# Norm products as chains of four passes, products of ones before two small chains, and steps of four generators set elsewhere, in a two-block float32 network on one core

## The chip, the cores and the metric

One core of one Trainium2 chip runs the whole program. The metric is the device time of one execution in microseconds; less is better. "TensorE" is the engine called PE in the profile, VectorE is DVE, ScalarE ACT, GpSimd POOL and SyncE SP.

## The reference

Two blocks work on 256 tokens of width 1,024, all in float32. The first block has four mixers side by side (retention, gated delta rule, gated linear attention and HGRN, four heads each), a cross attention to a memory of 256 tokens, and a feed forward with a causal convolution of width 3. The second block runs twice: three attentions side by side (latent, dilated, and a sparse one that picks keys by an index score), then a feed forward. Cut to what the change touches:

```python
def _rmsnorm(x, w):
    y = x * lax.rsqrt(jnp.mean(x * x, axis=-1, keepdims=True) + EPS)
    return y * w

def _conv_ffn(h, w_up, conv_w, w_down):                    # three times in all
    u = _causal_dwconv(jnp.matmul(h, w_up), conv_w)         # 1024 -> 2 x 2816
    gate, val = jnp.split(u, 2, axis=-1)
    return jnp.matmul(jax.nn.silu(gate) * val, w_down)      # 2816 -> 1024

def _gated_delta_chunked(q, k, v, beta, g):                 # chunks of 64
    ...
    u_v = lax.linalg.triangular_solve(a_mat, beta[..., None] * v, ...)
    ...

h = h + _hybrid_mixer(_rmsnorm(h, mix_norm_w[l]), ...)
h = h + _memory_cross_attn(_rmsnorm(h, xattn_norm_w[l]), _rmsnorm(mem, mem_norm_w), ...)
h = h + _conv_ffn(_rmsnorm(h, ffn_norm_w[l]), ...)

# sparse attention, per query block: an index score over 8 index heads, top 64 keys
score = jnp.einsum('bqhs,bqh->bqs', jax.nn.relu(dots), wib * idx_scale)
_, sel = lax.top_k(score, k_sel)
```

## The kernel before

Activations lie transposed: features on the 128 partitions, the 256 tokens along the columns, eight tiles for the width of 1,024. A float32 product is made of three: both operands are split into a high and a low part, and `mm_f` (L435 to L437) issues high by high, low by high and high by low into one PSUM bank, each a single pass over 256 columns. `mm_t` (L446 to L448) does the same with the tokens as rows. Products that are not split (`mm`, L457, and the transposes, L461) run on plain float32 and take two passes each.

Weights stream in 512 KB chunks. For each chunk the DMA on SP's queue loads `raw`, ScalarE makes the high part (L416) and VectorE the low part (L417), two chunks ahead of their use and at a higher priority (`PRIO = 42`) than other work on those engines.

A norm (`sumsq`, `mean`, `inv_root`) squares the eight tiles on ScalarE, adds them up on GpSimd (L540), and multiplies the sum by a matrix of ones on TensorE (`psS`, L457 from `mean`), which leaves each token's sum on all partitions. With `join=False` the last square is not added: `mean` then issues a second product of ones for it into the same bank. In `ffn` the first two of the 22 groups of the up projection (`FIRST = 2`) stand ahead of that product, everything else behind it; the result is only needed when the first groups are scaled.

The order of instructions on each engine is made by a scheduler from the order in which the program issues them, their dependences and their priorities. Where several chains run side by side they are Python generators, and `weave` takes one step of each in turn, up to its next `yield`. In the first block two such weaves follow each other: delta, HGRN and projections in turns (L779), then gated linear attention, the memory's norm (`keys_norm`) and retention (L782). `delta` solves its triangular system in five levels: per level a product `psy`, a masked copy `Y` on VectorE (L988), a product `psu`, an addition into `TM`, and a turn `psw` back through the identity. `scan_levels` makes for each of HGRN's levels scaled queries `R` on VectorE (L1133) and the product `psc`. `read_out` (bank `po`) sums a mixer's chunks; retention's comes behind its masked scores `Pm` (L1283). `keys` projects the memory to keys. In the second block a tuple, `ATTN`, sets the order of the attention's steps by hand; each "side" in it advances the top-k generator of the index score by one step, whose products are `psi` (L1619), with a rectifier on ScalarE (L1622) and an addition on VectorE behind them.

Of the kernel before, what the change touches and what calls it, by code (L numbers as in the profile page):

```python
# [22 lines left out]
EPS = 1e-6  # L23
NEG = -1e30
PRIO = 42
FIRST = 2
NZ = 4
LAST = 2
# [6 lines left out]
JOIN = True  # L35
ENG = False
STEP = 8
ATTN = ("kk", "qi0", "prep", "t0", "qi1", "uv", "uq0", "kp", "uq1", "ki", "mkb", "lv0", "uk0", "lv1", "tab", "side", "uq2", "M0",
        "uq3", "uk1", "l0", "Mv0", "M1", "Mv1", "D0", "Dv0", "l1", "l2", "side", "l3", "side", "D1", "Dv1", "side",
        "side", "D3", "side", "Dv3", "side", "D2", "side", "side", "s0", "sides", "Dv2", "s1", "S0", "S1", "Sv0",  # L40
        "Sv1")
MIX_ORDER = ("bq0", "bq1", "bk0", "bk1", "bv0", "bv1", "t0", "t1", "dq0", "dq1", "rq0", "rq1", "rk0", "rk1", "t3", "cq", "ck", "t2", "t4")
# [325 lines left out]
class Net:  # L368
# [87 lines left out]
    def mm(self, out, lhsT, rhs, start=True, stop=True):  # L456
        self.nc.tensor.matmul(out, lhsT, rhs, start=start, stop=stop, skip_group_check=True)  # L457

    def tr(self, out, in_):
        p = in_.shape[0]  # L460
        self.nc.tensor.transpose(out, in_, self.ident[:p, :p])  # L461
# [166 lines left out]
    def ffn(self, tag, g, fc, nt):  # L628
        nc = self.nc
        x = self.x  # L630
        xh, xl = self.xsplit(x, g)
        acc, = self.sumsq(x)
        with self.pool("ffn" + tag) as big, self.pool("fz" + tag, 3) as zp:
            self.pad(big, "g")
            gh = big.tile([P, NFF, T], F32R, name="gh")
# [217 lines left out]
    def delta(self, s, sm, gates):  # L853
# [25 lines left out]
        for t in range(2):  # L879
            for q, src in ((0, sq), (1, sk)):  # L880
                for i in range(2):
                    c = t * 8 + q * 4 + 2 * i
                    self.mm(ps[:, c:c + 2], src[:, i, t * P:(t + 1) * P], self.c1("hind"))
        rr = self.rsqrt(m, ps, 1.0, EPS, 16, "gd").rearrange("p (t q h) -> p t q h", t=2, q=2)
        cat = m.tile([P, 2, 3, 4], F32, name="cat")
        nc.vector.tensor_scalar(cat[:, :, 0, :], rr[:, :, 0, :], 0.125, None, ALU.mult)
        nc.vector.tensor_copy(cat[:, :, 1, :], rr[:, :, 1, :])
# [15 lines left out]
        bv = m.tile([P, 2, 4, 64], F32, tag="v", name="bv", bufs=3)  # L903
        for t in range(2):
            pv = self.pb(T, "psv")
            for i in range(2):
                self.tr(pv[:, i * P:(i + 1) * P], s[:, 4 + i, t * P:(t + 1) * P])
            nc.vector.tensor_mul(bv[:, t], pv.rearrange("p (h v) -> p h v", h=4),
                                 beta[:, t].unsqueeze(2).to_broadcast([P, 4, 64]))
# [68 lines left out]
        for k in range(1, 6):  # L978

            b = 1 << k  # L980
            left = lambda a: a.rearrange("p g (n c d) -> p g n c d", c=2, d=b)[:, :, :, 0, :]
            yield
            py = self.pb(T, "psy").rearrange("p (g n d) -> p g n d", g=8, d=b)
            for g in range(8):
                for r in halves:
                    self.mm(py[r, g], An[r, g // 4, g % 4, r], left(Tm)[r, g])
            Y = m.tile([P, 8, 32], F32, tag="Yl", name="Y")
            nc.vector.tensor_mul(Y, py.rearrange("p g n d -> p g (n d)"),  # L988
                                 self.c1("mko")[:, (k - 1) * 32:k * 32].unsqueeze(1).to_broadcast([P, 8, 32]))
            pu = self.pb(T, "psu2").rearrange("p (g c) -> p g c", g=8)  # L990
            for g in range(8):
                for r in halves:
                    self.mm(pu[r, g, :], Tx[r, g, :], Y[r, g, :])
            nc.vector.tensor_add(left(Tm), left(Tm), pu.rearrange("p g (n d) -> p g n d", d=b))
            yield
            turn(Tx, Tm)
# [34 lines left out]
    def read_out(self, i, Pm, v):  # L1031

        nc, m = self.nc, self.mp
        po = self.pso.tile([P, 2, T], F32, tag="o", name="po")
        for h in range(4):
            c = slice(h * 64, (h + 1) * 64)
            self.mm(po[:, 0, c], Pm[:, 0, h, :], v[:, 0, h, :])
            self.mm(po[:, 1, c], Pm[:, 2, h, :], v[:, 0, h, :], stop=False)
            self.mm(po[:, 1, c], Pm[:, 1, h, :], v[:, 1, h, :], start=False)
# [230 lines left out]
    def retention(self, xh, xl, gates, tmaj):  # L1270
# [7 lines left out]
        for h in range(4):  # L1278
# [3 lines left out]
                self.mm(ps[:, c0:c0 + n], k[r, h // 2, st * P:(st + 1) * P], q[r, h // 2, st * P:T], start=st == 0)  # L1282
            nc.vector.tensor_mul(Pm[:, 0::2, h, :], ps[:, 0:T].rearrange("p (b c) -> p b c", b=2), dec[:, h, :].rearrange("p (b c) -> p b c", b=2))  # L1283
            nc.vector.tensor_mul(Pm[:, 1, h, :], ps[:, T:384], dec[:, h, 0:P])
        self.read_out(0, Pm, vR)


    def keys_norm(self, mem):
        nc = self.nc
        nc.sync.dma_start(mem, self.ap["memT"])  # L1290
        self.pad(self.memp, "m")
        self.mh = self.memp.tile([P, KD, T], F32R, name="mh")
        self.ml = self.memp.tile([P, KD, T], F32R, name="ml")
        g = self.par("memw")
        for k in range(KD):
            self.split(self.mh[:, k, :], self.ml[:, k, :], mem[:, k, :], g[:, k:k + 1])
            if k % 2:
                yield
        acc, = self.sumsq(mem)
        yield  # L1300
        v, L = self.mean(acc, "irv")
        self.mB = self.inv_root(self.st, v, L, "nB")
        yield
        self.mT = self.cols(self.st, self.mB)

    def keys(self):
        nc = self.nc
        self.preload("natural_log_exp_and_others", self.last_silu)
        self.kM = self.memp.tile([P, KD, T], F32, name="kM")
        for i in range(KD):  # L1310
            ps = self.pa(T, "psk")
            self.mm_f(ps, f"wk{i}", range(KD), self.mh, self.ml)
            nc.scalar.copy(self.kM[:, i, :], ps)

    def xattn(self, es):
        nc = self.nc
# [293 lines left out]
    def topk(self, m, qi, ki, wi, sel):  # L1610
# [4 lines left out]
        for h in range(8):  # L1615
# [7 lines left out]
            for t in range(2):  # L1623
                prev = acc[:, sl[t]] if h else (cm[:, P:T] if t == 0 else cm)
                nc.vector.scalar_tensor_tensor(acc[:, sl[t]], rl[:, sl[t]], wi[:, t, h:h + 1], prev, ALU.mult, ALU.add)
            if h % 4 == 3:
                yield
        m8 = m.tile([P, 2, 8], F32, name="m8")
        out = -3.0e38
# [72 lines left out]
```

## Time and profile before

| | |
|---|---|
| median of three runs | 1159.55 us |
| the three runs | 1151.79, 1159.55, 1160.25 us |
| the profiled execution, its own time | 1151.56 us |
| its span in the trace | 1149.8 us, so 1.76 us lie around it |
| TensorE busy | 98% of the span |
| VectorE, ScalarE, GpSimd busy | 81%, 58%, 10% |
| mean granted clock of TensorE | 0.994 |
| read from memory | 182.07 MB, 159 GB/s over the span |

The trace gives each instruction's start and duration. Matmuls are pipelined, so a duration (0.28 us for a single pass of 256 columns) is longer than the distance to the next start; rates are read from starts or from counts in a window. A count x2 on a product of one call is its number of passes. PEclk is the granted clock as a share of the full 2.4 GHz.

### The profile page before, as it was taken

What the parts mean: (1) busy time and instruction counts of PE and PEld (TensorE: products, weight loads), DVE (VectorE), ACT (ScalarE), POOL (GpSimd) and SP (SyncE); (2) the same over time, 40 slices, a digit from 0 to 9 for tenths busy, and PEclk for the clock granted to TensorE, in tenths of its full rate; (3) what the DMA queues carried; (4) which work ended last, traced back from release to release, by engine and by line L of the source; (5) the groups of instructions that cost most, each with busy time, mean ns of one, the idle gap of its engine ahead of it and who ended that gap; (6) DMA issues with size and microseconds to landing.
All of it is one profiled execution on the core that took longest, in us unless ns stands there. A gap on an engine that the chain in (4) does not pass through costs nothing.

```text
span 1149.8 us, 23781 instructions
## 1 busy us (share of the span) xinstructions
PE 1124.8 (98%) x9452; PEld 1079.7 (94%) x9452; DVE 927.7 (81%) x1867; ACT 666.2 (58%) x1173; POOL 112.4 (10%) x139
## 2 busy tenths in 40 slices
PE   8899999999999999999999999999999999999996
PEld 8788888989999999999989999999999899999996
DVE  6977769587589997659997899986679979999854
ACT  6653545466576665555555676665555547666642
POOL 7401201010010000223000200001220002000000
PEclk9999999999999999999999999999999999999999
DMA  7513142556456555554424556555553235555552
GB/s 256 181 57 109 40 152 72 182 182 217 130 166 199 188 187 192 185 172 150 140 93 128 166 202 201 188 198 193 180 172 119 94 129 170 198 189 192 188 184 85
DMA packets 52095, 184.66 MB, mean 161 GB/s; under 512 B 6032, under 2 KB 6928, under 8 KB 51728
## 3 DMA queue, kind: packets, MB, share of 16 engines
q1 hardware_dynamic: 51264, 181.90, 48.6%
q8 instruction: 74, 1.21, 0.4%
q0 software_dynamic: 144, 0.59, 0.2%
q10 hardware_dynamic: 576, 0.66, 0.2%
q14 instruction: 37, 0.30, 0.1%
HBM read 182.07 MB, written 1.05 MB: 159 GB/s over the span
## 4 chain that ended last, share of the span: by engine, by line
PE 87%; DVE 7%; ACT 2%; DMA 1%; issue 1%; POOL 1%; SPq 0%; DVEq 0%; ACTq 0%; POOLq 0%
PE psU L437 11%; PE psU L435 11%; PE psU L436 11%; PE psD L435 5%; PE psD L436 5%; PE psD L437 5%; PE po L457 3%; PE psp L435 3%; PE psp L436 3%; PE psp L437 3%; PE psW L435 3%; PE psW L437 3%; PE psW L436 2%; DVE wlo L417 2%; PE pss L457 2%; PE pst L448 2%
## 5 line engine op out<-in xcount | busy, mean ns | idle before, releaser
L416 ACT ACTIVATE whi<-raw 128x1024 fp32r<-128x1024 f32 (+5 forms) x411 | 362.5, 898 | 298.3 <-PE psU L436 59.6
L417 DVE TENSOR_TENSOR wlo<-raw,whi 128x1024 fp32r<-128x1024 f32 (+5 forms) x411 | 425.6, 1048 | 133.2 <-ACT whi L416 130.3
L435 PE MATMUL psU<-xh,whi 128*128 128x256 f32 x1056 | 295.4, 280 | 0.0
L437 PE MATMUL psU<-xh,wlo 128*128 128x256 f32 x1056 | 295.0, 279 | 0.3 <-DVE wlo L417 0.3
L436 PE MATMUL psU<-xl,whi 128*128 128x256 f32 x1056 | 294.8, 279 | 0.0
L437 PEld LDWEIGHTS psU<-xh,wlo 128*128 128x128 f32 x1056 | 201.0, 190 | 0.5 <-DVE wlo L417 0.5
L436 PEld LDWEIGHTS psU<-xl,whi 128*128 128x128 f32 x1056 | 198.4, 188 | 0.1
L435 PEld LDWEIGHTS psU<-xh,whi 128*128 128x128 f32 x1056 | 198.2, 188 | 0.1
L437 PE MATMUL psD<-gh,wlo 128*128 128x256 f32 x528 | 147.5, 279 | 0.0
L435 PE MATMUL psD<-gh,whi 128*128 128x256 f32 x528 | 147.5, 279 | 0.0
L436 PE MATMUL psD<-gl,whi 128*128 128x256 f32 x528 | 147.5, 279 | 0.0
L540 POOL TENSOR_TENSOR ssa<-ssa,ssq 128x256 f32<-128x256 f32 x61 | 56.6, 932 | 692.4 <-ACT ssq L538 428.6
L673 DVE SCALAR_TENSOR_TENSOR y<-zb,prm,y 128x256 f32<-128x256 f32 x264 | 114.2, 480 | 0.0
L437 PEld LDWEIGHTS psD<-gh,wlo 128*128 128x128 f32 x528 | 100.6, 191 | 0.0
L436 PEld LDWEIGHTS psD<-gl,whi 128*128 128x128 f32 x528 | 99.1, 188 | 0.0
L435 PEld LDWEIGHTS psD<-gh,whi 128*128 128x128 f32 x528 | 99.1, 188 | 0.0
L435 PE MATMUL psp<-xh,whi 128*128 128x256 f32 (+1 forms) x288 | 83.5, 290 | 0.0
L436 PE MATMUL psp<-xl,whi 128*128 128x256 f32 (+1 forms) x288 | 82.4, 286 | 0.0
L437 PE MATMUL psp<-xh,wlo 128*128 128x256 f32 (+1 forms) x288 | 82.1, 285 | 0.0
L664 ACT ACTIVATE y<-zb,prm 128x256 f32<-128x256 f32 x132 | 67.3, 558 | 5.7 <-DVE zb L660 5.5
L446 PE MATMUL pst<-whi,xh 128*128 128x256 f32 (+3 forms) x176 | 56.9, 323 | 2.0 <-ACT gates L774 1.6
L435 PEld LDWEIGHTS psp<-xh,whi 128*128 128x128 f32 (+1 forms) x288 | 54.3, 188 | 2.4 <-issue 2.3
(452 smaller groups left out, 2305.4 us busy)
## 6 DMA issues: line engine op xcount, KB each, us to landing
raw<-in_wst_dram SPq DMA_DIRECT2D x319, 512.0 KB, 3.5
raw<-in_wst_dram SPq DMA_DIRECT2D x5, 448.0 KB, 3.3
cst<-in_c_dram SPq DMA_DIRECT2D x1, 1664.0 KB, 7.2
raw<-in_wst_dram SPq DMA_DIRECT2D x3, 396.0 KB, 3.0
mem<-in_memT_dram SPq DMA_DIRECT2D x1, 1024.0 KB, 6.1
raw<-in_wst_dram SPq DMA_DIRECT2D x2, 480.0 KB, 3.1
raw<-in_wst_dram SPq DMA_DIRECT2D x2, 420.0 KB, 3.5
raw<-in_wst_dram SPq DMA_DIRECT2D x2, 384.0 KB, 4.2
```

Source lines behind the costliest of these rows:

```text
L416: nc.scalar.activation(hi[:, a:b], raw[:, a:b], AF.Copy)
L417: nc.vector.tensor_sub(lo[:, a:b], raw[:, a:b], hi[:, a:b].bitcast(F32))
L435: nc.tensor.matmul(ps, wh, xh[:, k, :], start=s, stop=False, skip_group_check=True)
L436: nc.tensor.matmul(ps, wh, xl[:, k, :], start=False, stop=False, skip_group_check=True)
L437: nc.tensor.matmul(ps, wl, xh[:, k, :], start=False, stop=e, skip_group_check=True)
L446: nc.tensor.matmul(pss[t], xh[:, k, a], wh, start=i == 0, stop=False, skip_group_check=True)
L448: nc.tensor.matmul(pss[t], xh[:, k, a], wl, start=False, stop=i == n - 1, skip_group_check=True)
L457: self.nc.tensor.matmul(out, lhsT, rhs, start=start, stop=stop, skip_group_check=True)
L540: (eng or nc.gpsimd).tensor_add(acc, acc, sq)
L664: nc.scalar.activation(y[:, e, u, :], z[:, e, 2:], AF.Identity, scale=fc[:, c + 2:c + 3], **kw)
L673: nc.vector.scalar_tensor_tensor(y[:, e, u, :], zs[u][:, e, j:j + T], fc[:, c + j:c + j + 1], y[:, e, u, :], ALU.mult, ALU.add)
```

## The change

Seven edits, none of which changes a projection. In each of the three feed forwards the sum of squares is taken with `join=False`: one addition on GpSimd less, and a second product of ones. Delta's reciprocal root gets a priority of its own (`URGENT = 200`). A helper `hum` issues products of the ones matrix by itself into a bank that the next product overwrites: four ahead of delta's first transposes of values (`psv`), three ahead of retention's read-out (`po`). Delta's level gets a third `yield`, behind `Y`; retention gets one ahead of its read-out. `keys_norm` yields at every tile, and its sum of squares, mean and root move into `keys`, behind the first, fifth and seventh tile of keys. The top-k generator yields at every second index head (before: every fourth), and `ATTN` has two more "side" steps.

```diff
+URGENT = 200
@@
-ATTN = (... "tab", "side", "uq2", "M0",
-        "uq3", "uk1", "l0", ...
+ATTN = (... "tab", "side", "uq2", "side", "M0",
+        "uq3", "side", "uk1", "l0", ...
@@
+    def hum(self, ps, n):
+        for _ in range(n):
+            self.mm(ps[:, 0:P], self.ones, self.ones)
@@ def ffn
-        acc, = self.sumsq(x)
+        acc, = self.sumsq(x, join=False)
@@ def delta
-        rr = self.rsqrt(m, ps, 1.0, EPS, 16, "gd").rearrange("p (t q h) -> p t q h", t=2, q=2)
+        with self.tc.high_priority(offset=URGENT):
+            rr = self.rsqrt(m, ps, 1.0, EPS, 16, "gd").rearrange("p (t q h) -> p t q h", t=2, q=2)
@@
             pv = self.pb(T, "psv")
+            if t == 0:
+                self.hum(pv, 4)
@@
             nc.vector.tensor_mul(Y, py.rearrange("p g n d -> p g (n d)"), ...)
+            yield
             pu = self.pb(T, "psu2").rearrange("p (g c) -> p g c", g=8)
@@ def read_out
         po = self.pso.tile([P, 2, T], F32, tag="o", name="po")
+        if i == 0:
+            self.hum(po[:, 0], 3)
@@ def retention
+        yield
         self.read_out(0, Pm, vR)
@@ def keys_norm
+        self.mem = mem
...
             self.split(self.mh[:, k, :], self.ml[:, k, :], mem[:, k, :], g[:, k:k + 1])
-            if k % 2:
-                yield
-        acc, = self.sumsq(mem)
-        yield
-        v, L = self.mean(acc, "irv")
-        self.mB = self.inv_root(self.st, v, L, "nB")
-        yield
-        self.mT = self.cols(self.st, self.mB)
+            yield
@@ def keys
-        self.preload("natural_log_exp_and_others", self.last_silu)
+        pl = self.preload("natural_log_exp_and_others", self.last_silu)
...
             nc.scalar.copy(self.kM[:, i, :], ps)
+            if i == 0:
+                acc, = self.sumsq(self.mem)
+            elif i == 4:
+                self.pl = pl
+                v, L = self.mean(acc, "irv")
+                self.mB = self.inv_root(self.st, v, L, "nB")
+                self.pl = None
+            elif i == 6:
+                self.mT = self.cols(self.st, self.mB)
@@ def topk
-            if h % 4 == 3:
+            if h % 2:
                 yield
```

The change shifts the line numbers by one from the first edit on and by more behind the later ones. Three places in TensorE's order show what moves.

TensorE at the norm of the first feed forward, before (`psU` is the up projection, `psS` the product of ones):

```order
L436 MATMUL psU<-xl,whi 128x256
L437 MATMUL psU<-xh,wlo 128x256
L457 MATMUL psS<-ssa,ones 128x256
L435 MATMUL psU<-xh,whi 128x256
L436 MATMUL psU<-xl,whi 128x256
```

And now:

```order
L437 MATMUL psU<-xl,whi 128x256
L438 MATMUL psU<-xh,wlo 128x256
L458 MATMUL psS<-ssa,ones 128x256
L458 MATMUL psS<-ssq,ones 128x256
L436 MATMUL psU<-xh,whi 128x256
L437 MATMUL psU<-xl,whi 128x256
```

The second product of ones, for the last square, stands right behind the first; the stream of single passes around them is the same.

TensorE at the start of delta, before (`psr` turns the roots, `pse` spreads them, `psv` are the transposes of the values, `psq` and `pst` projections):

```order
L448 MATMUL pst<-wlo,xh 128x512
L435 MATMUL psq<-xh,whi 128x256
L436 MATMUL psq<-xl,whi 128x256
L461 MATMUL psr<-ident,cat 12x128 x2
L437 MATMUL psq<-xh,wlo 128x256
L435 MATMUL psq<-xh,whi 128x256
L436 MATMUL psq<-xl,whi 128x256
L437 MATMUL psq<-xh,wlo 128x256
L457 MATMUL pse<-rows,cst_142 128x256 x6
L461 MATMUL psv<-ident,s 128x128 x2
L435 MATMUL psq<-xh,whi 128x256
L461 MATMUL psv<-ident,s 128x128 x2
```

And now:

```order
L448 MATMUL pst<-whi,xl 128x512
L467 MATMUL psr<-ident,cat 12x128 x2
L449 MATMUL pst<-wlo,xh 128x512
L436 MATMUL psq<-xh,whi 128x256
L437 MATMUL psq<-xl,whi 128x256
L438 MATMUL psq<-xh,wlo 128x256
L436 MATMUL psq<-xh,whi 128x256
L437 MATMUL psq<-xl,whi 128x256
L438 MATMUL psq<-xh,wlo 128x256
L458 MATMUL pse<-rows,cst_142 128x256 x6
L458 MATMUL psv<-ones 128x128 x4
L467 MATMUL psv<-ident,s 128x128 x4
```

The turn of the roots now stands ahead of all of these `psq` products (before, behind two of them), so that six of them lie between it and `pse` instead of four; four products of ones stand ahead of the transposes, which follow each other without a projection between. Further on, delta's last three `psu`, two of its `psy` and three `psw` now stand with HGRN's `psc` and `psl` with only two `pst` products among them; before, runs of `psr` and `pst` lay between most of them.

TensorE in the first attention of the second block, where the index scores `psi` meet the latent projections `psp`, before:

```order
L448 MATMUL pst<-wlo,xh 128x256
L1619 MATMUL psi<-ki,qi 128x128
L1619 MATMUL psi<-ki,qi 128x256
L1619 MATMUL psi<-ki,qi 128x128
L1619 MATMUL psi<-ki,qi 128x256
L1619 MATMUL psi<-ki,qi 128x128
L1619 MATMUL psi<-ki,qi 128x256
L1619 MATMUL psi<-ki,qi 128x128
L1619 MATMUL psi<-ki,qi 128x256
L435 MATMUL psp<-lath,whi 128x256
```

And now:

```order
L449 MATMUL pst<-wlo,xh 128x256
L1635 MATMUL psi<-ki,qi 128x128
L1635 MATMUL psi<-ki,qi 128x256
L1635 MATMUL psi<-ki,qi 128x128
L1635 MATMUL psi<-ki,qi 128x256
L436 MATMUL psp<-lath,whi 128x256
L437 MATMUL psp<-latl,whi 128x256
L438 MATMUL psp<-lath,wlo 128x256
L436 MATMUL psp<-lath,whi 128x256
L437 MATMUL psp<-latl,whi 128x256
L438 MATMUL psp<-lath,wlo 128x256
L1635 MATMUL psi<-ki,qi 128x128
```

The products of four index heads, two each, stood in a row; now six projection products lie between the first two heads and the next two.

## Rows read from the trace of the kernel before

**Rows 1.** The page: busy time of each engine, its share, and instructions.
```profile
PE 1124.8 (98%) x9452; PEld 1079.7 (94%) x9452; DVE 927.7 (81%) x1867; ACT 666.2 (58%) x1173; POOL 112.4 (10%) x139
```

**Rows 2.** Windows: us, busy PE, PEld, DVE, ACT, POOL (x instructions), PEclk, DMA share, GB/s.
```profile
30.00:220.00 190.00, 182.10 (x1606) 161.31 (x1607) 149.88 (x358) 99.73 (x208) 26.68 (x31) 0.97 0.33 107
...
638.00:828.00 190.00, 190.00 (x1671) 189.80 (x1670) 160.18 (x233) 120.71 (x170) 15.75 (x19) 1.00 0.59 191
```

**Rows 3.** Windows, psU alone: us, PE, PEld, DVE, PEclk, DMA share, GB/s.
```profile
333.00:433.00 100.00, 100.00 (x851) 100.00 (x850) 13.23 (x20) 1.00 0.58 190
656.00:756.00 100.00, 100.00 (x885) 100.00 (x884) 13.04 (x19) 1.00 0.59 193
970.00:1070.00 100.00, 100.00 (x852) 100.00 (x850) 12.32 (x18) 1.00 0.57 189
```

**Rows 4.** Timeline of PE: start us, us, engine, line, operation, passes; around 514.53.
```profile
511.70 0.28 PE L435 MATMUL psp<-xh,whi 128*128 128x256 f32 x1
...
514.53 1.02 PE L457 MATMUL psS<-ssa,ones 128*128 128x256 f32 x4
...
515.51 0.28 PE L436 MATMUL psp<-xl,whi 128*96 128x256 f32 x1
...
515.98 0.28 PE L437 MATMUL psp<-xh,wlo 128*96 128x256 f32 x1
...
518.02 0.28 PE L437 MATMUL psp<-xh,wlo 128*96 128x256 f32 x1
```

**Rows 5.** Timeline of PE at the norms of the first and second feed forward.
```profile
330.36 0.59 PE L457 MATMUL psS<-ssa,ones 128*128 128x256 f32 x2
...
330.91 0.28 PE L436 MATMUL psU<-xl,whi 128*128 128x256 f32 x1
...
651.43 0.59 PE L457 MATMUL psS<-ssa,ones 128*128 128x256 f32 x2
```

**Rows 6.** Timeline of PE in the last attention.
```profile
901.09 0.93 PE L457 MATMUL pss<-rk,rq 64*128 64x128 f32 x8
...
902.75 0.28 PE L435 MATMUL psp<-xh,whi 128*128 128x256 f32 x1
...
904.34 0.28 PE L437 MATMUL psp<-xh,wlo 128*128 128x256 f32 x1
```

**Rows 7.** Windows at the two low clocks (columns as in rows 2).
```profile
53.30:60.10 6.80, 6.42 (x23) 5.15 (x22) 4.86 (x10) 0.76 (x2) 1.49 (x3) 0.50 0.23 77
131.80:135.20 3.40, 3.40 (x11) 2.45 (x10) 3.27 (x12) 0.00 (x0) 1.77 (x3) 0.50 0.00 0
```

**Rows 8.** Waits of PE: line waited for, us in total, times, longest us.
```profile
PE psi L1619 <- ACT irl L1622: 2.2, 3, 1.0
...
PE psc L457 <- DVE R L1133: 1.3, 2, 0.9
...
PE psu L457 <- DVE Y L988: 0.8, 2, 0.5
...
PE po L457 <- DVE Pm L1283: 0.7, 1, 0.7
PE psr L461 <- DVE cat L888: 0.6, 1, 0.6
```

**Rows 9.** Timeline of DVE and POOL at the memory's norm.
```profile
124.56 0.49 DVE L1133 TENSOR_TENSOR R<-qbD,Ehalf 128x128 f32<-128x128 f32 x2
...
127.07 5.62 POOL L540 TENSOR_TENSOR ssa<-ssa,ssq 128x256 f32<-128x256 f32 x7 [13.48 <-ACT ssq L538]
...
128.77 0.82 DVE L1133 TENSOR_TENSOR R<-qbD,Ehalf 128x128 f32<-128x128 f32 x1
```

**Rows 10.** Timeline of PE at one of delta's levels.
```profile
96.71 1.12 PE L457 MATMUL psy<-TM,An 64*64 64x32 f32 x32
...
100.34 1.12 PE L457 MATMUL psu<-Y,TM 64*64 64x32 f32 x32 [0.48 <-DVE Y L988]
```

More of the change, by code (lines that the diff above doesn't have):

```diff
@@ L37 @@
 STEP = 8
-ATTN = ("kk", "qi0", "prep", "t0", "qi1", "uv", "uq0", "kp", "uq1", "ki", "mkb", "lv0", "uk0", "lv1", "tab", "side", "uq2", "M0",
-        "uq3", "uk1", "l0", "Mv0", "M1", "Mv1", "D0", "Dv0", "l1", "l2", "side", "l3", "side", "D1", "Dv1", "side",
+ATTN = ("kk", "qi0", "prep", "t0", "qi1", "uv", "uq0", "kp", "uq1", "ki", "mkb", "lv0", "uk0", "lv1", "tab", "side", "uq2", "side", "M0",
+        "uq3", "side", "uk1", "l0", "Mv0", "M1", "Mv1", "D0", "Dv0", "l1", "l2", "side", "l3", "side", "D1", "Dv1", "side",
         "side", "D3", "side", "Dv3", "side", "D2", "side", "side", "s0", "sides", "Dv2", "s1", "S0", "S1", "Sv0",
```

## The prediction

> **What bounds the kernel now.** I read the busy line first. TensorE is busy 1,124.8 of 1,149.8 us [rows 1], so whatever the change gains has to come out of TensorE's own time: out of products that take longer than they need, or out of the 25 us in which it stands. The windows by stage come next [rows 2]. The stretch from 30 to 220 us holds the mixers and most of the edits; there TensorE stands 190.00 - 182.10 = 7.9 us, and its granted clock is 0.97. The stretch from 638 to 828 us is mostly a feed forward; there it does not stand at all and the clock is 1.00. The feed forwards therefore can't gain from waits.
>
> The third view is the same 100 us inside each of the three feed forwards [rows 3]. All three are 100% busy at clock 1.00 on the same kind of product (one pass, 256 columns), yet they start 851, 885 and 852 of them: 117.5, 113.0 and 117.4 ns each. That is two discrete spacings, not noise. Where the spacing changes is seen at the norm product of the second block [rows 4]: from 511.70 to 514.53 us there are 24 starts, 2.83 / 24 = 117.9 ns; then comes a chain of two products of ones, four passes; from 515.98 to 518.02 there are 18 starts, 113.3 ns. A product of two passes does it less reliably [rows 5]: the first feed forward's, at 330.36, was left wide, the second's, at 651.43, short. A chain of eight passes before a projection also ends short [rows 6]: 902.75 to 904.34, 14 starts, 113.6 ns. I read this as a spacing that any disturbance of the stream sets anew and that then stays: a single product of two passes sets it by luck, a chain of four and more mostly sets it short.
>
> **The change part by part**, against the profiled execution's own 1151.56 us (span 1149.8 and 1.76 around it). That execution is the fastest kind shown: the three runs read 1151.79, 1159.55 and 1160.25. The 8 us between the first and the other two are, as an estimate, little more than one feed forward in the other spacing (6.7, below), so I take the sum from this execution and compare the result with the median, 1159.55.
>
> A. Spacing in the feed forwards. The second product of ones makes the last disturbance of each feed forward a chain of four passes, like that of rows 4. A feed forward has 22 x 2 x 8 x 3 = 1,056 up products and 8 x 22 x 3 = 528 down products; 96 of them (two of 22 groups) stand ahead of the norm, 1,488 behind. By rows 3 the difference is 117.5 - 113.0 = 4.5 ns, so 6.7 us each. The first and third go from wide to short, the second is short already: -13.4. The bounds are 0 and -13.4. I take -13.4 since the one chain of this very form in the trace (rows 4) turned wide into short. Whether weights arrive in time at the shorter spacing is answered by the second feed forward: 885 products at a DMA share of 0.59 and TensorE still 100% busy [rows 3].
>
> B. Added products. From the norm product's start to the second single product behind it is 0.98 us with four passes (514.53 to 515.51, rows 4) and 0.55 with two (330.36 to 330.91, rows 5): +0.43 per feed forward, +1.3. The dropped POOL add, its last in each norm, only lets the norm product be ready earlier; TensorE does not wait there. The seven products ahead of delta's values and the first read-out are 14 passes of 128 columns; eight passes of 128 columns took 0.93 with their tail [rows 6], about 0.11 each, so +1.5 at full clock and +3.0 at half (bounds 0, where they fill a wait, and 3.0). They wait for the bank that the products behind them need anyway, so they bring no wait of their own, but all of TensorE's queue stands behind them. Together +2.8.
>
> C. Waits. The ones that the moved steps touch are five [rows 8]. The indexer's products (psi) wait 2.2 us for ACT's rectifier to empty a bank. The changed order puts six projection products, 6 x 0.113 = 0.7 us, between the first two index heads and the next two; three waits of up to 1.0 lose most of that: -1.5. The four of the mixers are 1.3 (psc behind R), 0.8 (psu behind Y), 0.7 (po behind Pm), 0.6 (psr behind cat), sum 3.4. The R waits come while POOL makes the seven adds of the memory norm: R takes 0.25 us apiece at 124.56 and 0.82 at 128.77, inside the adds of 127.07 to 132.69 [rows 9]. The change moves these adds into the memory keys' stream, where TensorE has 64 x 3 long products in hand. The root chain ahead, the extra step behind Y and the step ahead of the read-out each put other work in the gap of its own wait. I take -2.5 of 3.4. What is late next is delta itself: with an extra step per level the scan advances faster and eats the projections that stood between delta's later levels, so +1.0 of new waits. Sum -3.0; bounds -5.6 (all five gone) and +5 (none gone, and new ones of the size of the old).
>
> On rows 9 the Trainium skill ("SBUF — State Buffer", section "SBUF: two separate sides") says that VectorE and GpSimd share a port pair as an exclusive lock, which the one that starts first holds for its whole instruction. Row and rule agree (0.25 against 0.82), and the rule speaks against the move: beside the keys the adds block the weight conversions instead, up to the adds' own 5.6 us of VectorE. By it C would be -3.0 + 5.6 = +2.6 at worst; I leave it out of the sum because conversions run ahead of the products.
>
> D. Clock. Twice the granted clock falls to 0.50, the 1.2 GHz level: 53.3 to 60.1 and 131.8 to 135.2 us [rows 7], in both cases after TensorE had stood or run few and small products (the root's wait; the R waits). Half of each stretch is lost: 3.4 + 1.7 = 5.1. The added products of ones stand right at the first, and the moved adds take away the cause of the second. Bounds -5.1 and, since every shift of small work can also open a new dip of that size, +3.4; I take half, -2.5.
>
> Everything else (keys' norm products, the top-k steps, the retention step) is the same work in other places, at 0, hidden by a TensorE that is full around it; no DMA moves with these steps (the memory's load stays where it was). If that cover were gone, the two norm products and two transposes of the memory would cost the 0.55 us of rows 5 twice, 1.1.
>
> Sum: -13.4 + 2.8 - 3.0 - 2.5 = -16.1, so 1135.5 us.
>
> **The rivals.**
>
> Only one of the two wide feed forwards turns short, or the second turns wide while two turn short: -6.7 instead of -13.4, 1142.2 us. For it: a product of two passes left either spacing, and rows 4 are one case only.
>
> The second product does not act on the spacing (it is set elsewhere, or the same luck goes on): A is 0, time 1148.9. [...] Against this rival also speaks that the change of spacing in rows 4 falls exactly on the chain.
>
> The chain sets the wide spacing, everywhere: nothing gained, and the second feed forward loses its short one, 1148.9 + 6.7 = 1155.6.
>
> The slow side: delta's last levels. In the changed order three levels and half of the scan stand in a row with hardly a projection between: some 13 pieces like the 1.12 us psu of rows 10, and 2.4 us of scan products (estimate), 17 us. Between psy (ends 97.83) and psu (100.34) a level's values need 2.5 us to come back from VectorE [rows 10]; a 1.1 us piece covers less than half, so eight hand-overs may each wait 1.4, 11 us, and such a stretch is just what went before the dips of rows 7: at half clock another 17. 1135.5 + 28 = 1164, slower than the 1159.55 median. It decides from 24 us of loss on. Against it: the scan's own waits in this trace are 1.3 and 0.8 in sum [rows 8], and VectorE is relieved there.
>
> The added products of ones do not hold the clock: D is 0, 1138.0; it lies in the forecast's range.
>
> **How the numbers follow.** Forecast 0.50 and its variant without D 0.03; one feed forward only 0.20; no effect on the spacing 0.15; wide everywhere 0.05; delta's levels 0.07. The range goes down to 1129 (all of C, D and no cost of the products of ones would give 1151.56 - 13.4 + 1.3 - 5.6 - 5.1 = 1128.8) and up to 1150, which takes in the case without an effect on spacing. A measurement of this kernel can tell about 1%, 11.6 us, from no change, so faster means below 1147.9, against the median of 1159.55: the first two cases and most of a third of the no-effect case, less what C may give back, 0.74; same 0.21; slower 0.05.
>
> **What would show it.** Right: some 885 psU products per 100 us in all three feed forwards, at 113 ns, each behind a psS of four passes; psi and psc gone from the head of TensorE's waits; clock 1.00 from 50 to 61 and around 130 us. Wrong: 851 per 100 us in a feed forward behind a four-pass psS kills A; new waits of psu, psw or psy or a clock of 0.50 where delta's levels run is the slow rival.

## The result

The change is faster by 1.2%: 1144.26 us, median of four runs (1141.30 to 1146.34), against 1158.9 us before (four runs, 1151.79 to 1160.25); ratio 0.9884, 95% interval 0.9838 to 0.993. The profiled execution took 1141.30 us, 10.3 less than the one profiled before. Ratios, here and below, leave out executions more than 1.5% above the fastest of their kernel, so that they can differ from the ratio of the medians. The forecast of 1135.5 was too far, its range of 1129 to 1150 held, and in the profiles the gain is its term A. The other six edits together gave nothing.

The busy line of the page after, against [rows 1]:

```profile
PE 1113.3 (98%) x9472; PEld 1067.9 (94%) x9472; DVE 926.7 (81%) x1867; ACT 666.6 (58%) x1173; POOL 109.8 (10%) x136
```

TensorE has 20 instructions more and 11.5 us less busy time: its products became shorter in distance, not fewer. Where, the windows of `psU` show, which answer to [rows 3] (us, PE, PEld, DVE, clock, DMA share, GB/s):

```profile
333.00:433.00 100.00, 100.00 (x885) 100.00 (x884) 13.61 (x20) 1.00 0.61 194
656.00:756.00 100.00, 99.66 (x880) 99.46 (x878) 13.03 (x19) 1.00 0.61 197
970.00:1070.00 100.00, 99.68 (x880) 99.48 (x878) 13.00 (x19) 1.00 0.60 194
```

All three feed forwards now run at 113 ns; before, two of the three stood at 851 and 852. The weights arrive in time for it (DMA share 0.60 against 0.58). The norm's chain in the first feed forward (timeline of PE; against the first two of [rows 5]):

```profile
330.51 0.28 PE L438 MATMUL psU<-xh,wlo 128*128 128x256 f32 x1
330.62 0.59 PE L458 MATMUL psS<-ssa,ones 128*128 128x256 f32 x2
331.06 0.59 PE L458 MATMUL psS<-ssq,ones 128*128 128x256 f32 x2
331.30 0.47 PE L436 MATMUL psU<-xh,whi 128*128 128x256 f32 x1
```

The waits, against [rows 8] (us in total, times, longest):

```profile
PE psc L458 <- DVE R L1132: 1.4, 1, 1.4
...
PE psr L458 <- DVE Pm L1296: 1.0, 1, 1.0
...
PE psr L467 <- DVE cat L895: 0.8, 1, 0.8
...
PE psi L1635 <- ACT irl L1638: 0.4, 1, 0.4
```

The index scores wait 0.4 us instead of 2.2, and `psu` behind `Y` is gone from the list. But other waits took the places: the `R` of the other scan's last level (L1132; the line that was L1133 is L1145 now, and waits 0.3) 1.4, the retention scores behind `Pm` 1.0 (before, the read-out behind it 0.7), the roots' turn 0.8 (0.6).

To see where the time went, each execution was cut at the starts of some of TensorE's instructions in its trace: the first `pse`, the first `psy`, the first `psW` (the mixers' output), the first `psU` and last `psD` of each feed forward. A column gives the length from the place before it (the first from the span's start); "FFN" runs from the first `psU` to the last `psD`, "attention" from there to the next `psU`. Lengths in us, worked out from these starts, one execution a row:

| kernel | to pse | to psy | to psW | to psU | FFN 1 | attention | FFN 2 | attention | FFN 3 |
|---|---|---|---|---|---|---|---|---|---|
| before | 51.3 | 17.9 | 144.0 | 104.6 | 188.2 | 133.5 | 181.0 | 131.2 | 187.9 |
| after | 53.0 | 17.5 | 142.1 | 105.4 | 182.0 | 134.2 | 181.0 | 132.4 | 181.7 |
| after_again | 54.1 | 18.8 | 142.0 | 105.7 | 182.0 | 135.9 | 181.0 | 132.2 | 181.7 |
| ffn_only | 51.7 | 17.5 | 143.8 | 105.6 | 188.8 | 133.4 | 181.0 | 133.1 | 182.1 |
| no_ffn | 53.0 | 18.6 | 142.0 | 105.5 | 188.2 | 134.9 | 187.1 | 132.0 | 187.9 |
| ffn_halves | 53.5 | 18.5 | 147.4 | 104.2 | 188.0 | 133.4 | 180.6 | 132.8 | 181.3 |
| no_hum | 54.3 | 18.8 | 140.0 | 104.4 | 182.0 | 136.0 | 188.0 | 132.1 | 181.7 |
| old_attn | 52.8 | 17.5 | 142.2 | 105.7 | 182.1 | 133.4 | 181.0 | 133.5 | 181.7 |
| old_keys | 53.9 | 18.7 | 140.2 | 105.5 | 188.8 | 134.7 | 188.0 | 132.2 | 188.7 |
| no_y_step | 53.8 | 18.5 | 146.2 | 105.5 | 182.1 | 133.8 | 181.0 | 132.7 | 181.7 |
| ffn_six | 53.9 | 17.5 | 142.3 | 105.3 | 182.4 | 134.2 | 181.4 | 132.1 | 182.1 |
| ffn_eight | 52.7 | 17.5 | 142.1 | 105.8 | 182.9 | 134.2 | 181.8 | 132.8 | 182.5 |
| mix_hum | 53.0 | 18.2 | 140.0 | 105.5 | 182.0 | 133.2 | 181.0 | 133.0 | 181.7 |
| mix | 54.7 | 17.8 | 138.5 | 104.9 | 182.0 | 133.2 | 181.0 | 130.9 | 181.7 |

Between the first two rows: 12.4 us less in the feed forwards, 1.9 less in the mixers' stretch ("to psW"), 4.1 more in the others. The six kernels whose mixers are those of the whole change agree within 0.3 us in the mixers' stretch (142.0 to 142.3). The start, the stretch to psy and the first attention differ by 1.1 to 1.7 us between after and after_again, which are the same code, so a difference of that size in one of these is not told from chance.

### The profile page after: what moved, and what is told of

It reads as the page before. It is cut to its first block, busy times and chain, and to the rows that moved or that the text cites. A ratio compares the mean times of both kernels' runs of the same rounds, so it can differ in the third digit from the quotient of the medians.

```text
span 1139.5 us, 23807 instructions
## 1 busy us (share of the span) xinstructions
PE 1113.3 (98%) x9472; PEld 1067.9 (94%) x9472; DVE 926.7 (81%) x1867; ACT 666.6 (58%) x1173; POOL 109.8 (10%) x136
## 4 chain that ended last, share of the span: by engine, by line
PE 84%; DVE 11%; ACT 2%; DMA 1%; issue 1%; POOL 0%; SPq 0%; DVEq 0%; ACTq 0%
PE psU L438 10%; PE psU L436 10%; PE psU L437 10%; PE psD L438 5%; PE psD L436 5%; PE psD L437 5%; DVE wlo L418 4%; PE po L458 3%; PE psW L436 3%; PE psW L438 3%; PE psW L437 2%; PE psp L436 2%; PE psp L438 2%; PE psp L437 2%; PE pst L449 2%; PE pst L447 2%
## 5 line engine op out<-in xcount | busy, mean ns | idle before, releaser
L436 PE MATMUL psU<-xh,whi 128*128 128x256 f32 x1056 | 292.1, 277 | 0.0
L438 PE MATMUL psU<-xh,wlo 128*128 128x256 f32 x1056 | 291.6, 276 | 0.3 <-DVE wlo L418 0.3
L437 PE MATMUL psU<-xl,whi 128*128 128x256 f32 x1056 | 291.5, 276 | 0.0
L438 PEld LDWEIGHTS psU<-xh,wlo 128*128 128x128 f32 x1056 | 198.2, 188 | 0.5 <-DVE wlo L418 0.5
L546 POOL TENSOR_TENSOR ssa<-ssa,ssq 128x256 f32<-128x256 f32 x58 | 53.1, 920 | 681.1 <-ACT ssq L544 459.5
L670 ACT ACTIVATE y<-zb,prm 128x256 f32<-128x256 f32 x132 | 67.4, 560 | 11.5 <-DVE zb L666 11.3
L449 PE MATMUL pst<-wlo,xh 128*128 128x256 f32 (+3 forms) x176 | 55.0, 316 | 1.3 <-DVE wlo L418 1.3
```

Source lines behind the costliest of these rows:

```text
L436: nc.tensor.matmul(ps, wh, xh[:, k, :], start=s, stop=False, skip_group_check=True)
L437: nc.tensor.matmul(ps, wh, xl[:, k, :], start=False, stop=False, skip_group_check=True)
L438: nc.tensor.matmul(ps, wl, xh[:, k, :], start=False, stop=e, skip_group_check=True)
L449: nc.tensor.matmul(pss[t], xh[:, k, a], wl, start=False, stop=i == n - 1, skip_group_check=True)
L546: (eng or nc.gpsimd).tensor_add(acc, acc, sq)
L670: nc.scalar.activation(y[:, e, u, :], z[:, e, 2:], AF.Identity, scale=fc[:, c + 2:c + 3], **kw)
```

## The experiments

Two theories. The spacing: the second product of ones makes the gain. Its rival: the edits in the mixers and the attention make it. And against the reason for the spacing: that it is luck.

**The second product alone, and all but it.** `ffn_only` is the kernel before with one edit, `no_ffn` the whole change without it.

```diff
 # ffn_only: only this; no_ffn: everything but this
-        acc, = self.sumsq(x)
+        acc, = self.sumsq(x, join=False)
```

> The kernel before with one edit of the change, the second product of ones in the three feed forwards. If the spacing behind a chain of four passes is the gain: some 885 psU products per 100 us in all three feed forwards, a profiled time near 1151.6 - 13.4 + 1.3 = 1139.5 us, so no slower than the whole change (1141 to 1146). If the gain came from the mixers and the attention: 1150 to 1160, with 851 per 100 us in one feed forward at least.

> The whole change without the second product in the feed forwards. If the spacing is the gain: the feed forwards fall to either spacing by chance, 1141 to 1142 - 1.3 plus 6.7 for each wide one, so 1146 to 1160 and a spread of several us between executions; at three wide ones no faster than before. If the gain came from the other edits: 1140 to 1146, whatever the spacing.

> The whole change once more on this chip, to compare with the others: 1141 to 1146 us; 885 psU products per 100 us in all three feed forwards if the four passes set the spacing, 851 in one of them now and then if it is luck.

Measured: ffn_only 1145.84 us (1139.93 to 1149.04; ratio to before 0.9893, 0.986 to 0.9926), no_ffn 1162.31 (1154.41 to 1164.93; 1.0038, 1.0013 to 1.0064), after_again 1143.67 (1141.55 to 1145.38; 0.9872, 0.9837 to 0.9907). One edit gives what all seven give, and the other six alone are a little slower than before. The windows of psU in no_ffn:

```profile
333.00:433.00 100.00, 100.00 (x851) 100.00 (x850) 13.02 (x19) 1.00 0.56 189
656.00:756.00 100.00, 100.00 (x851) 100.00 (x850) 13.00 (x19) 1.00 0.55 188
970.00:1070.00 100.00, 99.92 (x848) 99.72 (x847) 12.24 (x18) 1.00 0.56 188
```

Wide in all three. But the expectation for ffn_only failed in one place; its windows:

```profile
333.00:433.00 100.00, 100.00 (x851) 100.00 (x850) 13.02 (x19) 1.00 0.55 188
656.00:756.00 100.00, 100.00 (x885) 100.00 (x884) 13.52 (x20) 1.00 0.57 193
970.00:1070.00 100.00, 100.00 (x884) 100.00 (x884) 13.60 (x20) 1.00 0.57 194
```

Its first feed forward stayed wide behind a chain of four passes. So a chain of four does not simply set the short spacing. The stream had turned wide 6 us ahead of the chain, where TensorE waits for a weight's low part (timeline of PE):

```profile
324.34 0.28 PE L437 MATMUL psU<-xh,wlo 128*128 128x256 f32 x1
...
325.25 0.28 PE L436 MATMUL psU<-xl,whi 128*128 128x256 f32 x1
325.81 0.39 PE L437 MATMUL psU<-xh,wlo 128*128 128x256 f32 x1 [0.29 <-DVE wlo L417]
326.03 0.28 PE L435 MATMUL psU<-xh,whi 128*128 128x256 f32 x1
...
327.09 0.28 PE L435 MATMUL psU<-xh,whi 128*128 128x256 f32 x1
```

From 324.34 to 325.25 are eight starts of 0.114 us, from 326.03 to 327.09 nine of 0.118. By their starts, eleven of the fourteen profiles have this gap with a short stream ahead of it: the stream turned wide there in ffn_only and old_keys and stayed short in the other nine. So the gap can turn it, and does not always.

**Four passes without a second operand.** `ffn_halves` is the kernel before with the one product of the feed forwards cut in two (`cut` is 2 there, 1 elsewhere).

```diff
-            self.mm(ps, self.ones, a, start=i == 0, stop=i == len(acc) - 1)
+            for c in range(cut):
+                b = slice(c * T // cut, (c + 1) * T // cut)
+                self.mm(ps[:, b], self.ones, a[:, b], start=i == 0, stop=i == len(acc) - 1)
```

> The kernel before; in the feed forwards the one product of ones is cut into two of 128 columns, so that four passes stand there with the same work and no second operand. If four passes set the short spacing: 885 per 100 us in all three, near 1139 us, less than ffn_only by the passes saved (0.4 us each). If 256 columns or the second operand are needed: 851 per 100 us in some, 1150 to 1160.

Measured: 1144.79 us (1139.76 to 1151.73; 0.9892, 0.9851 to 0.9933). Behind all three chains the spacing was short at first; in the first feed forward it turned wide 11 us later, behind a gap of 0.2 us (timeline of PE):

```profile
347.71 0.28 PE L436 MATMUL psU<-xl,whi 128*128 128x256 f32 x1
347.91 0.39 PE L437 MATMUL psU<-xh,wlo 128*128 128x256 f32 x1
348.14 0.28 PE L435 MATMUL psU<-xh,whi 128*128 128x256 f32 x1
...
348.96 0.28 PE L436 MATMUL psU<-xl,whi 128*128 128x256 f32 x1
```

From 348.14 to 348.96 are seven starts of 0.117 us. A short gap can come with a change of spacing too; one of 0.22 us at 348.56 in no_y_step left it short. Neither a second operand nor 256 columns are needed for the chain: three streams that came in short left four passes of 128 columns short. And the profiled execution's 1151.73 comes from this gap and from a mixers' stretch of 147.4, in which the clock was lower (5.0 us lost between 150 and 175).

**The edits beside it.** Four kernels, each the whole change without one edit.

```diff
 # no_hum
-            if t == 0:
-                self.hum(pv, 4)
-        if i == 0:
-            self.hum(po[:, 0], 3)
 # old_attn: ATTN as before, and
-            if h % 2:
+            if h % 4 == 3:
 # old_keys: keys_norm and keys as before
 # no_y_step, in delta's level
-            yield
             pu = self.pb(T, "psu2")
```

> The whole change without the seven products of ones. If these hold the clock (term D): the granted clock falls to 0.50 near 53 to 60 us for longer, and the stretch from pse to the first psy grows from 17.5 to 18.8 us by one or more. If they only cost: that stretch shrinks by about 1.5 and the time by as much, 1142.

> The whole change with the attention order and the top-k steps of before. If those edits gave the 1.5 us of psi waits: the two attention stretches (end of psD to the next psU; 134.2 to 135.9 and 132.0 to 132.4 with the change) grow by 0.7 each. If they cost more elsewhere: the stretches shrink to before's 133.5 and 131.2, and the time falls by 2 to 3 us, 1141.

> The whole change with the memory's norm back in keys_norm. If moving it gave the gain in the mixers: the stretch from the first psy to the first psW grows from 142.0 to 144 us, with R waits of 1 us and more and a clock of 0.50 near 130 us. If it is the step behind Y that gave it, the stretch stays at 142.

> The whole change without the extra step behind Y in delta's levels. If that step gave the gain in the mixers: the stretch from the first psy to the first psW goes from 142.0 back to 144 us. If it costs (the rival on delta's last levels): 141 or less. If the keys' move gave the gain: 142 stays.

Medians: no_hum 1145.91 us (1138.30 to 1155.24; ratio 0.9925, 0.9877 to 0.9973), old_attn 1141.60 (1140.65 to 1142.51; 0.9892, 0.9836 to 0.9948), old_keys 1154.07 (1138.70 to 1162.81; 0.9951, 0.9901 to 1.0002), no_y_step 1153.46 (1146.52 to 1160.70; 0.9994, 0.9954 to 1.0034). These medians mix the edit with the spacing, which moves a run by 6.7 us per feed forward: old_keys' profiled execution had all three wide, no_hum's one. The stretches tell the edits apart.

The extra step behind `Y` is the one of the edits tried that gains: without it the mixers' stretch is 146.2 instead of 142.0 us. The view of DVE and POOL in no_y_step shows why; against [rows 9]:

```profile
128.79 0.48 DVE L1144 TENSOR_TENSOR R<-qbD,Ehalf 128x128 f32<-128x128 f32 x2
...
131.29 5.63 POOL L546 TENSOR_TENSOR ssa<-ssa,ssq 128x256 f32<-128x256 f32 x7 [13.49 <-ACT ssq L544]
...
133.00 0.82 DVE L1144 TENSOR_TENSOR R<-qbD,Ehalf 128x128 f32<-128x128 f32 x1
```

The seven adds of the memory's norm stand beside the R exactly as before, although the keys' move is in this kernel. In the whole change (same view) the R are over before the adds begin:

```profile
108.97 1.30 DVE L1145 TENSOR_TENSOR R<-qbD,Ehalf 128x128 f32<-128x128 f32 x6 [0.54 <-PE psl L458]
...
115.04 4.15 POOL L546 TENSOR_TENSOR ssa<-ssa,ssq 128x256 f32<-128x256 f32 x5
```

Six R in 1.30 us, 0.22 each. So the step behind Y, which lets the scan run ahead of delta, parted R and adds; the keys' move left the adds where they were (in old_keys, without the move, they run at 117.10 us, behind the R as well). The waits of no_y_step bear it out:

```profile
PE psc L458 <- DVE R L1144: 2.1, 4, 0.9
...
PE psu L458 <- DVE Y L997: 1.2, 2, 0.9
```

The keys' move costs: with the old keys the stretch is 140.2 instead of 142.1 (140.0 in mix_hum, below). It brings the wait of 1.4 us for R of L1132, which stands, at 1.4 each time, in the lists of all eight kernels with the moved keys and in none of the six with the old ones. DVE and POOL at that place in the whole change:

```profile
183.53 4.05 POOL L798 TENSOR_TENSOR gates<-gates,prm 128x512 f32<-128x512 f32 x3 [61.10 <-ACT gates L795]
...
186.37 1.76 DVE L1132 TENSOR_TENSOR R<-qbC,Ehalf 128x512 f32<-128x512 f32 x1
```

And in old_keys:

```profile
187.43 4.86 POOL L798 TENSOR_TENSOR gates<-gates,prm 128x512 f32<-128x512 f32 x3 [62.95 <-ACT gates L795]
...
188.41 1.04 DVE L1132 TENSOR_TENSOR R<-qbC,Ehalf 128x512 f32<-128x512 f32 x1
```

The same R takes 1.76 us where it starts 2.8 us into POOL's three products and 1.04 where it starts 1.0 us into them; with no product on POOL the other scan's took 0.68 (at 113.32 us in the whole change). That the overlap is the cause was not tried by itself.

The products of ones cost 2.1 us in the mixers' stretch (142.1 with, 140.0 without; with the keys and the attention of before, in mix_hum and mix below, 1.5) and did nothing for the clock that the stretches show: the stretch from pse to psy is 17.5 to 18.8 us with them and without them alike. Their place tells why, in the timeline of PE of the whole change:

```profile
53.03 2.85 PE L458 MATMUL pse<-rows,cst 12*128 12x256 f32 x12
56.80 1.54 PE L458 MATMUL psv<-ones 128*128 128x128 f32 x8 [0.92 <-DVE qkb L907]
58.14 1.06 PE L467 MATMUL psv<-ident,s 128*128 128x128 f32 x4
```

They wait for the same bank as the products behind them (0.92 us, for VectorE to empty `pse`), so they start only when the idle time is over. The windows there, and at the second place of [rows 7]:

```profile
56.00:57.00 1.00, 0.20 (x1) 0.20 (x2) 1.00 (x3) 0.00 (x0) 0.00 (x0) 1.00 0.00 0
57.00:58.00 1.00, 1.00 (x8) 1.00 (x8) 1.00 (x3) 0.00 (x0) 0.00 (x0) 0.71 0.72 164
58.00:59.00 1.00, 1.00 (x7) 1.00 (x7) 1.00 (x2) 0.00 (x0) 0.00 (x0) 0.50 0.82 332
...
125.00:140.00 15.00, 15.00 (x92) 12.97 (x92) 10.51 (x38) 7.20 (x15) 0.00 (x0) 1.00 0.24 72
```

TensorE stands, and the clock falls to its 1.2 GHz level while the products of ones run. The second low clock is gone, and so are the waits for R there. That the one brought the other is not shown: in no_y_step the waits for R are longer (2.1 us, before 1.3), and the granted clock is 1.00 from 100 to 220 us.

The attention edits cost in the first attention: 133.2 to 133.5 us in the six kernels with the old order, 133.8 to 136.0 in the eight with the new; in the second no difference can be told (130.9 to 133.5 and 132.0 to 132.8). The 1.8 us won at psi is in the list of waits and not in the stretch. The priority and the retention step were not tried by themselves.

**What the chain does.** With the traces of ten kernels read, the spacing ahead of a feed forward's chain and behind it can be counted. Behind two passes a short stream was wide in 4 of 4 cases, and of two wide ones one came out short. Behind four a short stream stayed short in 17 of 17, and a wide one stayed wide in 5 of 7. One theory for it was that each further pair of passes turns the spacing round. In the feed forwards `more` is 1 in ffn_six and 2 in ffn_eight, in the whole change otherwise unaltered.

```diff
         ps = self.pb(T, "psS")
+        for _ in range(more):
+            self.mm(ps, self.ones, acc[0])
```

> The whole change with three products of ones in each feed forward, the first overwritten: six passes. So far a chain of two passes turned a short stream wide (4 of 4) and a chain of four left it short (17 of 17). If the number of passes turns the spacing round in steps of two: short ahead becomes wide behind, 851 psU products per 100 us, 1158 to 1166 us. If a longer chain simply keeps or sets the short spacing: 885, about 1145.

> The whole change with four products of ones in each feed forward: eight passes. If the passes turn the spacing round in steps of two, eight act as four: short stays short, 885 per 100 us, 1144 plus the added passes (3 x 0.86), 1146. If longer chains set the short spacing from either side, a feed forward that comes in wide leaves short as well, and the spread between executions goes.

Measured: ffn_six 1143.97 us (1143.22 to 1144.76; 0.9867, 0.9817 to 0.9918), ffn_eight 1144.34 (1143.91 to 1145.48; 0.9872, 0.9822 to 0.9922). The windows of ffn_six:

```profile
333.00:433.00 100.00, 100.00 (x884) 100.00 (x884) 13.57 (x20) 1.00 0.57 194
656.00:756.00 100.00, 100.00 (x884) 100.00 (x884) 12.99 (x19) 1.00 0.57 195
970.00:1070.00 100.00, 100.00 (x885) 100.00 (x884) 13.00 (x19) 1.00 0.58 195
```

Six passes keep the short spacing like four, so the turning round in steps of two is false. Each further product costs 0.4 us per feed forward (182.0, 182.4, 182.9). All six streams of these two profiles came in short, so whether a longer chain makes a wide stream short stays open. That four passes keep a wide stream wide is seen in old_keys, where all three came in wide and left wide; its first:

```profile
330.43 0.28 PE L436 MATMUL psU<-xh,whi 128*128 128x256 f32 x1
...
331.14 0.59 PE L458 MATMUL psS<-ssa,ones 128*128 128x256 f32 x2
331.57 0.59 PE L458 MATMUL psS<-ssq,ones 128*128 128x256 f32 x2
...
332.12 0.28 PE L437 MATMUL psU<-xl,whi 128*128 128x256 f32 x1
...
333.18 0.28 PE L437 MATMUL psU<-xl,whi 128*128 128x256 f32 x1
```

From 330.43 to 331.14 are six starts of 0.118 us, and from 332.12 to 333.18 nine of 0.118. The first stream of ffn_only and the second of no_hum did the same.

These counts hold for the feed forwards alone. The attentions of the second block have such norms too, with four passes in the first attention and two in the second. Behind them the stream was short in all 28 cases of the fourteen profiles, also where it came in wide, five times ahead of four passes and three times ahead of two. One of the latter, in no_hum (timeline of PE):

```profile
829.68 0.28 PE L436 MATMUL psp<-xh,whi 128*128 128x256 f32 x1
...
832.03 0.28 PE L438 MATMUL psp<-xh,wlo 128*128 128x256 f32 x1
832.16 0.59 PE L458 MATMUL psS<-ssa,ones 128*128 128x256 f32 x2
...
832.71 0.28 PE L437 MATMUL psp<-xl,whi 128*96 128x256 f32 x1
...
834.19 0.28 PE L438 MATMUL psp<-xh,wlo 128*96 128x256 f32 x1
```

From 829.68 to 832.03 are 20 starts of 0.118 us, from 832.71 to 834.19 thirteen of 0.114. So the number of passes does not decide by itself. What is different here is that the products behind the chain have weights of 96 columns (128*96) instead of 128; no stream of these was wide in any profile. Whether that form or the chain makes them short was not tried.

**A version of the parts that gain.** `mix` has the second product, delta's priority, the step behind Y and the retention step, and attention, top-k and keys as before; `mix_hum` also has the products of ones.

```diff
 # against the whole change
 # mix_hum: ATTN, topk, keys_norm and keys as before
 # mix: the same, and
-                self.hum(pv, 4)
-            self.hum(po[:, 0], 3)
```

> The second product, the priority, the step behind Y, the retention step and the products of ones; attention, top-k and keys as before. By the stretches so far (first psy to psW 140.2 with the old keys against 142.0; attention 0.5 to 2 less): 1137 to 1141 where all three feed forwards are short, 6.7 more for each wide one.

> As mix_hum, without the seven products of ones. If these only cost (140.0 against 142.0 in the stretch from the first psy to psW without them): 1136 to 1139 where all three feed forwards are short, faster than the whole change. If the two savings are one and the same: as mix_hum.

Measured: mix_hum 1143.14 us (1139.18 to 1152.15; 0.9871, 0.981 to 0.9932), mix 1139.79 (1135.90 to 1145.44; 0.9841, 0.979 to 0.9891). The profiled executions, both with all three feed forwards short, took 1139.65 and 1136.82 against 1141.30 of the whole change. The intervals of mix and of the whole change (0.9838 to 0.993) overlap; the stretches don't hinge on the spacing of the feed forwards and show 3.6 us less between the first psy and the first psW. By its median mix is the fastest of the kernels run.

## Why the prediction was right, and where it was wrong

**What bounds the kernel.** Right: TensorE's busy time fell by 11.5 us and the time by 10.3.

**A, the spacing.** The size was right: 188.2 to 182.0 and 187.9 to 181.7 us, -12.4 in sum, where A and its share of B gave -13.4 + 1.3 = -12.1; the second feed forward, short in both profiles, stayed at 181.0. The reason was wrong in part. The prediction read rows 4 as "a chain of four and more mostly sets it short". In the feed forwards two passes turned a short stream wide in 4 of 4 cases, and four left it short, in 23 of 23 once mix_hum and mix are counted; of the seven wide streams ahead of four passes only two came out short. So there the chain keeps a short spacing and mostly does not make one. And rows 4 could not show what was read from them: the products behind that chain are of the form 128*96, those ahead 128*128, and streams of 128*96 are short in every profile, behind two passes as behind four.

Before, one of the three streams came in short (the first) and was turned wide by the two passes. In the two profiles of the whole change all six came in short, so that term A came out whole is in part luck. That luck lies ahead of the norm, in the 96 products and the output projection before them; the wait at 325.81 in ffn_only is one place of it. That ffn_only, no_hum and old_keys still spread over 9 to 24 us fits this, but only their profiled executions show which spacing they had. What makes a stream come in short is open.

It may explain the medians as well. On the chip of the first experiments the kernel before measured 1145.06 and 1146.55, then 1152.96 to 1154.61, then 1157.04 to 1159.44 in 16 of its 17 runs. As an estimate from the profile (1151.56 with two wide feed forwards, 6.7 us each) one, two and three wide ones make 1144.9, 1151.6 and 1158.3. On the chip of the next experiments its 25 runs lie between 1145 and 1165 without such groups, so this is argued and not shown. The profiled execution of before was faster than most, so the medians moved by more (14.6) than the profiles (10.3).

**B.** Right for the feed forwards (0.4 each, as ffn_six and ffn_eight show again). For the products of ones +1.5 was forecast; +2.1 (no_hum) and +1.5 (mix) were measured in the mixers' stretch alone, which holds only the three of the read-out; six passes of some 0.11 us explain 0.7 of it. The rest goes with the order around them (the way from psy to retention's scores, ahead of the read-out, is 1.1 to 1.2 us shorter without them) and was not traced to an instruction.

**C, waits, is the step that failed.** -3.0 was forecast. The mixers' stretch gave -1.9, and the attentions, the start and the keys took 4.1, not all of it told from chance. Three parts of it were wrong. "The change moves these adds into the memory keys' stream" was wrong: the scheduler had them ready early and ran them at 115 us; it was the step behind Y, for which the prediction counted the wait of `psu` alone, that parted R from them. The rival on delta's last levels, slower by that very step, is refuted: without it the stretch is 4.2 us longer, in one profile against six that agree. And "-1.5" for psi holds for the wait and not for the time: TensorE then waits elsewhere in the attentions, 1.8 us behind `vS` and `as` where it was 0.5. The new waits were put at +1.0; the one for R of L1132 alone is 1.4.

On the port: rows 9 and the two R of L1132 agree with the rule that the Trainium skill gives ("SBUF — State Buffer", section "SBUF: two separate sides") that the two engines lock each other out. The danger that the prediction named, adds beside the weight conversions, did not come up as such. But where the adds went they stand beside the splits of the memory, in the whole change (timeline of DVE):

```profile
116.83 5.88 DVE L477 SCALAR_TENSOR_TENSOR ml<-mem,prm,mh 128x256 fp32r<-128x256 f32 x7
```

That is 0.84 us each; before, six of them took 2.45 us at 122.20, 0.41 each, ahead of the adds. TensorE did not feel it: it is busy for all of the 25 us from 100 to 125.

**D, the clock.** The second low clock went (-1.7). Which edit did it is not settled: no_hum, old_keys and no_y_step are all without it, and ffn_halves, with none of these edits, had it later and longer (150 to 175 us). The first stayed: by the windows from 20 to 62 us it cost 1.7 us in the whole change, 4.2 in its repetition and 3.4 before, and 1.7 in ffn_only, which has no products of ones. The step that failed is "the added products of ones stand right at the first": they stand behind the wait that comes ahead of the fall.

**The start.** The stretch to the first pse is 51.3 and 51.7 us in before and ffn_only, but 53.5 in ffn_halves, which has the same code there; with the priority 52.7 to 54.7 in eleven profiles. A cost of the priority of some 1 us is possible and was not tried alone.

The rivals: no effect on the spacing, and wide everywhere, are refuted by no_ffn against after_again. One wide feed forward, the next rival, is what the profiles of ffn_only, no_hum and ffn_halves show with the chain of four in place. The likeliest case was the right one, 5.8 us too low against the profiled execution, all of it from C, D and the products of ones.

## What to carry to other kernels

Count the products per 100 us in every long stream of equal products, not only its busy share: two streams at 100% can differ by 4%. Look at what interrupts such a stream last before its long part; a lone short interruption cost this kernel 6.7 us per stream, and doubling it, at 0.4 us, was the whole gain. Before you read a cause from one place of a trace, see whether anything else changes there, such as the form of the products. A filler product only bridges idle time if it can start when the idle time starts: in a bank that the waiting work needs too, it waits with the work it should bridge (a bank of its own was not tried here).

When executions of one kernel spread by more than an edit is worth, judge small edits by stretches of the trace rather than by medians, and when you shift one chain look first at which engine it will now meet.

## What was not expected of the hardware

The single products of 256 columns have two spacings at a granted clock of 1.00, 113.0 and 117.5 ns by the counts in the windows (113.3 and 117.8 by the starts; a window also counts products that only reach into it), which can hold for a whole feed forward's 1,488 products. In the feed forwards two passes of ones turned a short stream wide in 4 of 4 cases; four, six and eight left it short in 23, 3 and 3 of as many. Products with weights of 96 columns were short in all 28 streams. Why is not shown by any run.
